# A layer's up and down products by seven: PSUM tiles of their own, a pinned matmul order, and another order of the seven

## The chip, the cores and the metric

The kernel runs on one core of a Trainium2 chip. Its time is the device time in microseconds (us) of one launch, and the median over runs counts.

## The reference

One step of a one-layer encoder on 576 tokens (a prompt of 512 and a sample of 64 with a cache of 128 rows), D_MODEL = 1024, D_FF = 4096, all in float32:

```python
def finish_layer(x, mix, pe, w_o, ln1_g, ln1_b, w_up, w_down, ln2_g, ln2_b, w_ple, w_ple_gate, b_ple_gate):
    x = layer_norm(ALPHA * x + jnp.einsum('blm,md->bld', mix, w_o), ln1_g, ln1_b)
    hid = jnp.square(jax.nn.relu(jnp.einsum('bld,df->blf', x, w_up)))
    x = layer_norm(ALPHA * x + jnp.einsum('blf,fd->bld', hid, w_down), ln2_g, ln2_b)
    gate = jax.nn.sigmoid(jnp.einsum('bld,de->ble', x, w_ple_gate) + b_ple_gate)
    return x + gate * jnp.einsum('blp,pd->bld', pe, w_ple)
```

`mix` comes from two kinds of attention over a joint projection of x; the change does not touch them. What it touches is the first layer norm and the two large products of the feed-forward part, w_up and w_down.

## The kernel before, in words

**Engines.** TensorE (PE) multiplies, VectorE (DVE) and ScalarE (ACT) do the steps between, SyncE (SP) issues most loads, GpSimd (POOL) some loads and a few sums. A float32 product is made of three matmuls in a rounded format: high part by high part, high by low, low by high. So each weight goes from its raw tile (`wraw`) into a tile `whl` with a high part, cast by ACT (line 149), and a low part, raw minus high, by DVE (line 155). The `whl` tiles are a ring of five slots. A slot is taken again when the weights that it held have been used.

**Stages.** Projection, attention, output product (`wo1`, `wo2`), first layer norm, up group 0 and 1 by plain products, then the phase of this change, `seven(todo)`, then a plain down part, the second layer norm and the gate. In PSUM there are eight banks: two tiles of two banks with tag "m" (pool psM), one tile of two banks with tag "g" (psB), and two banks of the pool psN.

**The seven-product phase.** Tokens are cut in two halves A and B of HW = 288 columns, the contracted dimension in two, the outputs in two. By a scheme like Strassen's, a block product that needs eight multiplications is made with seven, on sums and differences of the operands. The seven are called 11, t0, t1, 21, t3, t2 and 22. Each is four blocks of the contracted dimension times three matmuls, so 12 matmuls of 128x128 by 288 columns, and each has its own operand (`ROWS`: t0 uses the set s3, t1 s2, t3 s1, 21 the set 12, t2 the set 22, 22 the set s4). The sets of the hidden values lie in tiles hA (s3 and 11), hB (12 and 22), hC (s1 and s2) and hD (s4); `operands` makes them from hF and r (lines 1326 to 1356). A pair of output blocks runs through all seven:

- o = 11, then + t1, then + t2, in one accumulation;
- d begins as a copy of o after 11 (ACT, line 1466), then + 21;
- e begins as minus o after t1 (ACT, line 1468), then + t3 and + 22;
- z = t0.

DVE and ACT then add these into Y (a down pair, lines 1551 to 1571) or make relu and square of them (an up pair, lines 1524 to 1543). A pair's weights are four units u0 to u3 in four `whl` slots, two products to a slot except the last (`PLACE`): 11 and 21 in u0, t0 and t3 in u1, t1 and t2 in u2, 22 in u3. DVE makes the sums of raw weights (lines 181 and 184).

The list `todo` has 24 pairs in six stages of four: down (group 1), up (2 and 3), down (3), up (4 and 5), down (5), up (6 and 7). Together 24 × 7 × 12 = 2016 matmuls.

**PSUM in the phase.** o and z are the two banks of one tile `P.oz`: alternately the psN tile N2 and the psB tile. d and e are the two banks of a psM tile `P.sz`. The source's order in a pair is t0, t1, 21, t3, t2, 11 of the next pair, 22.

**What sets the order.** The source writes steps as generators; small work on ACT and DVE is put in a list (`later`, `owe`) and taken between matmuls. A scheduler then orders each engine's instructions by priorities and a cost model, and keeps the source's order only for instructions that are marked with `tc.keep_in_program_order`. Before, no matmul of `gemm` is marked.

Of the kernel before, what the change touches and what calls it, by code (L numbers as in the profile page):

```python
# [31 lines left out]
HW = NT // 2  # L32
# [4 lines left out]
def tile_hybrid_step(ctx: ExitStack, tc: tile.TileContext, I, O):  # L37
    nc = tc.nc
    PE, ACT, DVE, POOL, SP = nc.tensor, nc.scalar, nc.vector, nc.gpsimd, nc.sync
# [67 lines left out]
    class Unit:  # L107


        def __init__(self, t, c, o=0):  # L110
            self.t, self.c, self.o = t, c, o
# [166 lines left out]

    WT = Weights()

    def gemm(ps, W, kmap, aH, aL, cols, yield_every=6, first=True, last=True, wc=slice(0, 128), k0=0, more=False):

        n = len(kmap) * 3
        i = 0
        for kw, ka in enumerate(kmap, k0):
            for w, a in ((0, aH), (0, aL), (1, aH)):
                PE.matmul(ps, W(w, kw, wc), a[:, ka, cols], start=(first and i == 0), stop=(last and i == n - 1),  # L287
                          skip_group_check=more)
                i += 1
                if i % yield_every == 0:  # L290
                    yield 1
# [5 lines left out]
    psM = ctx.enter_context(tc.tile_pool(name="psM", bufs=1, space=PS))  # L297
# [56 lines left out]
    U = {}  # L354
# [355 lines left out]
    def proj_evac(p, kind, m):  # L710
        g, pp = divmod(p, 4)
        v = m[:, :, :HW]
        P = pair[p]
        dly = [0]

        def q(fn, d=None):
            if d is not None:
                dly[0] = d
            later(dly[0], fn)
# [5 lines left out]
        if kind == "v":  # L725
            v32 = sb.tile([128, NT], F32, name="v32", tag="t1")
            q(lambda: ACT.copy(v2(v32), v))
            P["v32"] = v32
            return
        QE = sb.tile([128, NT], F32R, name=kind + "E", bufs=2)  # L730
        QO = sb.tile([128, NT], F32R, name=kind + "O", bufs=2)
        P[kind + "E"], P[kind + "O"] = QE, QO
        sc = -0.125 if kind == "q" else 1.0
        if g == 0:
            if kind == "q":
                P["q32s"] = QS[p % 2]
                P["Q2"] = Q2[p % 2]

# [333 lines left out]
    for x, tag in ((0, "k32"), (1, "t2")):  # L1072
        t = sb.tile([128, NT], F32, name="praw", tag=tag)
# [34 lines left out]
    psN = ctx.enter_context(tc.tile_pool(name="psN", bufs=1, space=PS))  # L1108
    psB = ctx.enter_context(tc.tile_pool(name="psB", bufs=1, space=PS))
# [8 lines left out]
    turn = [0]  # L1118
# [4 lines left out]
            return psB.tile([128, 2, 512], F32, name="g", tag="g", bufs=1)  # L1123
        return psM.tile([128, 2, 512], F32, name="g", tag="m", bufs=2)

    N2 = psN.tile([128, 2, 512], F32, name="n", tag="n", bufs=1)
    turn_n = [0]

    def psum_n():
        turn_n[0] ^= 1  # L1130
        return N2[:, turn_n[0]]

    unit_w = WT.use

# [310 lines left out]
    ROWS = {"11": "11", "t3": "s1", "t0": "s3", "21": "12", "t1": "s2", "22": "s4", "t2": "22"}  # L1445

    def seven(pairs):

        def product(P, n):
            if n == "11":  # L1450
                P.oz = N2 if P.i % 2 == 0 else psB.tile([128, 2, 512], F32, name="g", tag="g", bufs=1)
            elif n in P.starts:
                P.starts[n]()
            x = P.X[ROWS[n]]
            while owed.get(ROWS[n]) and P.X is HX:
                pop_now()
            bank = {"11": (P.oz, 0), "t1": (P.oz, 0), "t2": (P.oz, 0), "t0": (P.oz, 1)}.get(n)
            t, o = bank or (P.sz, 0 if n == "21" else 1)
            ps, first = t[:, o, :HW], n in ("11", "t0")
            W = WT.quarter(P.u, n, oldest[0])  # L1460
            for _ in gemm(ps, W, range(4), x[0], x[1], slice(0, HW), first=first, more=not first):
                WT.step()
                yield 1
            if n == "11":
                P.sz = psM.tile([128, 2, 512], F32, name="g", tag="m", bufs=2)
                ACT.copy(P.sz[:, 0, :HW], ps)
            elif n == "t1":
                ACT.mul(P.sz[:, 1, :HW], ps, -1.0)  # L1468
            if n in P.posts:
                P.posts[n]()  # L1470
            for k, name in (("21", 1), ("t3", 2), ("t2", 3), ("22", 4)):
                if n == k:
                    oldest[0] = P.u + name

        oldest = [pairs[0].u]
        yield from product(pairs[0], "11")
        for i, P in enumerate(pairs):
            names = ["t0", "t1", "21", "t3", "t2", "22"]
            names.insert(1 if i == 0 else 5, "11")
            for n in names:  # L1480
                if n != "11":
                    yield from product(P, n)
                elif i + 1 < len(pairs):
                    yield from product(pairs[i + 1], n)

    class Pair:

        made = 0

        def __init__(self, u, X):  # L1490
            self.u, self.X, self.i = u, X, Pair.made
            self.starts, self.posts, self.left = {}, {}, 0
            Pair.made += 1
# [12 lines left out]
    def v2(G):  # L1506
        return G[:, :, :HW]

    def up_pair(g, m):

        P = Pair(U["P", g // 2, g % 2 * 2 + m], SX)
        b = slice(2 * m, 2 * m + 2)
        tt = DVE.tensor_tensor
        if m == 0:
            P.starts["t0"] = lambda: sets(g)

        def bank(n):
            return {"o": P.oz[:, 0, :HW], "z": P.oz[:, 1, :HW], "d": P.sz[:, 0, :HW], "e": P.sz[:, 1, :HW]}[n]

        def target(t):  # L1520
            return HX["f"][:, t, b] if g < G_DOWN and g % 2 == 0 else P.r[:, t]

        def t0():
            P.r = fs.tile([128, 2, 2, HW], F32, name="r", bufs=2)
            owe(P, lambda: ACT.copy(P.r[:, 1, 0], bank("z")))  # L1525

        def t3():
            settle(P)
            tt(P.r[:, 1, 1], bank("e"), P.r[:, 1, 0], OP.subtract)

        def t2():
            tt(P.r[:, 1, 0], bank("o"), P.r[:, 1, 0], OP.add)
            later(0, lambda: ACT.activation(P.r[:, 1], P.r[:, 1], AF.Relu))
            later(0, lambda: ACT.activation(target(1), P.r[:, 1], AF.Square))
            operands(g, m, 1, target(1))

        def s22():
            if g % 2:
                later(0, lambda: DVE.tensor_scalar(P.r[:, 0], v2(P.sz), 0.0, None, op0=OP.max))
            else:  # L1540
                later(0, lambda: ACT.activation(P.r[:, 0], v2(P.sz), AF.Relu))
            later(0, lambda: ACT.activation(target(0), P.r[:, 0], AF.Square))
            operands(g, m, 0, target(0))
        P.posts = {"t0": t0, "t3": t3, "t2": t2, "22": s22}
        return P

    def down_pair(g, c):

        P = Pair(U["Q", g // 2, c], HX)
        tt, stt = DVE.tensor_tensor, DVE.scalar_tensor_tensor  # L1550
        s = ALPHA if g == 1 else 1.0
        ya, y01, y11 = Y[:, 2 * c:2 * c + 2, A], Y[:, 2 * c, B], Y[:, 2 * c + 1, B]

        def begin(y, ps, op):
            if s == 1.0:
                tt(y, y, ps, op)
            else:
                stt(y, y, s, ps, op0=OP.mult, op1=op)

        def t0():  # L1560
            owe(P, lambda: begin(y01, P.oz[:, 1, :HW], OP.add))
            owe(P, lambda: begin(y11, P.oz[:, 1, :HW], OP.subtract))

        def t3():
            settle(P)
            tt(y11, y11, P.sz[:, 1, :HW], OP.add)

        def t2():
            later(0, lambda: tt(y01, y01, P.oz[:, 0, :HW], OP.add))

        def s22():
            later(0, lambda: begin(ya, v2(P.sz), OP.add))
        P.posts = {"t0": t0, "t3": t3, "t2": t2, "22": s22}
        return P

    def down_last(sl, ln):
# [223 lines left out]
```

## Time and profile before

| | us |
|---|---|
| median of 3 runs (lowest, highest) | 807.86 (807.19, 808.79) |
| profiled execution, its own time | 808.51 |
| its span | 806.7 |
| PE busy | 769.9 |
| DVE busy | 580.6 |
| ACT busy | 471.1 |
| POOL busy | 110.6 |
| seven-product phase, from 383.9 to 698.6 | 314.7 |

All times in views are from the span's start. A row of the timeline gives start, length, engine, line, operation, output and input, and how many instructions it groups. In square brackets is the idle time of the engine just ahead and what ended it. Rows of one engine overlap a little, since the end of an instruction lies behind the start of the next; what a step costs its engine is the distance from start to start.

### The profile page before, as it was taken

Reading aid. Unit: us, or ns where it says so; the run is one execution under the profiler, and the core shown is the slowest. Engines: PE = TensorE matmul, PEld = TensorE weight load, DVE = VectorE, ACT = ScalarE, POOL = GpSimd, SP = SyncE. Lnnn points to the kernel's source line nnn. Section 1 sums busy time; section 2 is a strip of 40 time slices with the busy share of each in tenths; the row PEclk is TensorE's granted clock in tenths of the full one; section 3 lists DMA queues with packets and bytes.
Section 4 is the critical chain, followed back from the end, with each engine's and each line's share of the span. In section 5 each row is a group of like instructions: output and inputs, shape, how many; then the busy total and the mean of one; then the engine's idle time right before and its main releaser. Section 6 shows DMA issues by size and latency. Waiting matters only on the chain.

```text
span 806.7 us, 14678 instructions
## 1 busy us (share of the span) xinstructions
PE 769.9 (95%) x5679; PEld 740.1 (92%) x5679; DVE 580.6 (72%) x1146; ACT 471.1 (58%) x927; POOL 110.6 (14%) x130
## 2 busy tenths in 40 slices
PE   9999999999999999999799997999979999999997
PEld 7999989989999999899699997999969999999997
DVE  6788898797778669986575678656795666558753
ACT  5689777877767343975433575435763365634552
POOL 7001324334420001000000000000000000010100
PEclk9999999999999999999799998999999999999999
DMA  8547444363233232536065664567554763651001
GB/s 277 167 60 174 118 120 124 96 200 107 84 87 100 74 123 103 193 75 149 0 161 131 166 165 110 125 151 182 146 131 101 174 162 91 243 183 53 28 27 66
DMA packets 38198, 101.36 MB, mean 126 GB/s; under 512 B 6000, under 2 KB 10224, under 8 KB 38000
## 3 DMA queue, kind: packets, MB, share of 16 engines
q1 hardware_dynamic: 34384, 87.61, 35.4%
q0 software_dynamic: 3456, 12.58, 9.7%
q8 instruction: 45, 0.74, 0.4%
q10 hardware_dynamic: 288, 0.22, 0.1%
q14 instruction: 25, 0.20, 0.1%
HBM read 85.26 MB, written 9.54 MB: 118 GB/s over the span
## 4 chain that ended last, share of the span: by engine, by line
PE 74%; DVE 14%; ACT 9%; issue 3%; DMA 1%; ACTq 0%; DVEq 0%
PE g L287 42%; PE m L287 14%; PE n L287 8%; ACT whl L149 2%; PE T L56 2%; PE V L955 2%; DVE dbias L690 2%; ACT xr L768 1%; DVE m L688 1%; DVE whl L155 1%; PE m L449 1%; PE S L880 1%; PE S L878 1%; DVE sP L888 1%; PE m L463 1%
## 5 line engine op out<-in xcount | busy, mean ns | idle before, releaser
L155 DVE TENSOR_TENSOR whl<-wraw,whl 128x1024 fp32r<-128x1024 f32 (+2 forms) x158 | 158.5, 1012 | 110.7 <-ACT whl L149 109.8
L149 ACT CAST whl<-wraw 128x1024 fp32r<-128x1024 f32 (+2 forms) x190 | 155.1, 828 | 114.7 <-PE g L287 89.9
L287 PE MATMUL g<-BH,whl 128*128 128x288 f32 (+2 forms) x864 | 181.4, 298 | 0.7 <-ACT whl L149 0.4
L287 PE MATMUL m<-AH,whl 128*128 128x288 f32 x736 | 176.7, 307 | 0.0
L287 PEld LDWEIGHTS g<-BH,whl 128*128 128x128 f32 x864 | 140.9, 188 | 3.7 <-ACT g L1468 2.5
L287 PE MATMUL g<-BL,whl 128*128 128x288 f32 (+2 forms) x432 | 127.6, 295 | 1.5 <-DVE BL L1221 1.5
L287 PEld LDWEIGHTS m<-AH,whl 128*128 128x128 f32 x736 | 126.4, 188 | 1.7 <-issue 1.0
L287 PE MATMUL m<-AL,whl 128*128 128x288 f32 x368 | 108.7, 295 | 0.0
L287 PEld LDWEIGHTS g<-BL,whl 128*128 128x128 f32 x432 | 81.4, 188 | 2.1 <-DVE BL L1221 2.0
L287 PEld LDWEIGHTS m<-AL,whl 128*128 128x128 f32 x368 | 69.5, 189 | 0.6
L210 POOL DMA_DIRECT2D wraw<-in_w_dram x24 | 20.7, 863 | 326.9 <-DMA wraw<-in_w_dram 219.7
L893 ACT ACTIVATE sP<-sP,st 128x128 f32<-128x128 f32 (+4 forms) x72 | 39.4, 550 | 35.4 <-DVE st L888 35.3
L155 POOL TENSOR_TENSOR whl<-wraw,whl 128x512 fp32r<-128x512 f32 x32 | 42.2, 1334 | 90.2 <-ACT whl L149 74.9
L287 PE MATMUL g<-s,whl 128*128 128x288 f32 x288 | 42.4, 296 | 0.8 <-ACT r L1525 0.8
L287 PE MATMUL m<-BH,whl 128*128 128x288 f32 x192 | 42.9, 302 | 0.0
L287 PE MATMUL g<-hB,whl 128*128 128x288 f32 x216 | 36.9, 325 | 6.3 <-ACT g L1468 6.3
L287 PEld LDWEIGHTS g<-hB,whl 128*128 128x128 f32 x216 | 33.2, 211 | 9.4 <-ACT g L1468 9.4
L287 PEld LDWEIGHTS g<-s,whl 128*128 128x128 f32 x288 | 39.3, 188 | 1.6 <-ACT r L1525 1.5
L287 PE MATMUL g<-hC,whl 128*128 128x288 f32 x216 | 34.6, 306 | 0.0
L56 PE MATMUL T<-ident,sP 128*128 128x128 f32 (+1 forms) x176 | 31.3, 273 | 1.5 <-DVE sP L902 0.6
L287 PEld LDWEIGHTS m<-BH,whl 128*128 128x128 f32 x192 | 32.0, 188 | 0.5 <-issue 0.3
L287 PEld LDWEIGHTS g<-hC,whl 128*128 128x128 f32 x216 | 31.5, 198 | 0.6
(329 smaller groups left out, 1567.7 us busy)
## 6 DMA issues: line engine op xcount, KB each, us to landing
wraw<-in_w_dram SPq DMA_DIRECT2D x48, 512.0 KB, 3.6
wraw<-in_w_dram POOLq DMA_DIRECT2D x24, 512.0 KB, 5.7
wraw<-in_w_qkv_dram SPq DMA_DIRECT2D x23, 512.0 KB, 3.6
wraw<-in_w_dram SPq DMA_DIRECT2D x24, 256.0 KB, 4.1
wraw<-in_w_up_dram SPq DMA_DIRECT2D x8, 512.0 KB, 4.4
wraw<-in_w_down_dram SPq DMA_DIRECT2D x8, 512.0 KB, 4.2
wraw<-in_w_gate_dram SPq DMA_DIRECT2D x8, 512.0 KB, 4.5
wraw<-in_w_o_dram SPq DMA_DIRECT2D x8, 384.0 KB, 3.1
```

Of the source, the lines that this page charges most:

```text
L56: PE.transpose(out, in_, ident[:n, :n])
L149: ACT.copy(self.hv[u][:, 0, c], src["tile"][:, c])
L155: eng.tensor_tensor(t[:, 1, c], src["tile"][:, c], f(t[:, 0, c]), OP.subtract)
L210: POOL.dma_start(t[:, :n], it["acc"], accum_op=OP.add)
L287: PE.matmul(ps, W(w, kw, wc), a[:, ka, cols], start=(first and i == 0), stop=(last and i == n - 1), skip_group_check=more)
L449: PE.matmul(mk[:, h, :HW], w0(part, k), a[:, k, h * HW:(h + 1) * HW], start=(k == 0 and i == 0), stop=(k == 7 and i == 2))
L463: PE.matmul(acc[b][:n[b], :304], a[:, k, b * 128:b * 128 + n[b]], ixw(part, k), start=(k == 0 and i == 0), stop=(k == 7 and i == 2))
L688: tc.keep_in_program_order(DVE.max(m, s))
L690: tc.keep_in_program_order(DVE.match_replace(out=s, in_to_replace=m, in_values=s, imm_value=GONE))
L768: q(lambda r=r, s=s: ACT.mul(v2(xr[r * 32:r * 32 + 32]), v[s * 32:s * 32 + 32], sc))
L893: ACT.activation(j["P"], j["P"], AF.Exp, bias=j["st"][:, 0:1], scale=-1.0, accum_out=j["st"][:, 2:3])
L955: PE.matmul(ps[r, x * 256 + c.start:x * 256 + c.stop], P["vt"][:, kb, r], t[:, hh, kb, c], start=(kb == 0), stop=(kb == n - 1))
```

## The change

Four things, all in the feed-forward part:

1. The matmuls of the seven-product phase are marked to stay in the source's order (`pin=True`).
2. Each of o, z, d, e gets its own place. o is a tile of one bank from psN (two of them, `psum_n`), z is bank 0 of the psB tile. In most pairs d and e are still the two banks of a psM tile. In a "turn" pair, the first of each down stage, d is the second bank of the psB tile and e the second bank of the psM tile, and d is added into Y after 21, without waiting for 22.
3. The source's order of the seven becomes 21, t1, 11 of the next pair, t3, t2, t0 of the next pair, 22; in a turn pair 11 of the next, t1, 21, t3, t2, t0 of the next, 22. The first pair begins with 11 and t0.
4. In odd up groups relu and square behind t2 are one DVE instruction (line 1529 in the new program) in place of two on ACT, and relu behind 22 is on ACT where it was on DVE.

The first layer norm uses `psum_n` too, so its sums lie in two tiles of one bank where they were the two halves of one tile.

```diff
-    def gemm(ps, W, kmap, aH, aL, cols, ..., k0=0, more=False):
+    def gemm(ps, W, kmap, aH, aL, cols, ..., k0=0, more=False,
+             pin=False):
...
-                PE.matmul(ps, W(w, kw, wc), a[:, ka, cols], ...)
+                mm = PE.matmul(ps, W(w, kw, wc), a[:, ka, cols], ...)
+                if pin:
+                    tc.keep_in_program_order(mm)
...
-    N2 = psN.tile([128, 2, 512], F32, name="n", tag="n", bufs=1)
-    turn_n = [0]
     def psum_n():
-        turn_n[0] ^= 1
-        return N2[:, turn_n[0]]
+        return psN.tile([128, 512], F32, name="n", tag="n", bufs=2)
...
         def product(P, n):
             if n == "11":
-                P.oz = N2 if P.i % 2 == 0 else psB.tile([128, 2, 512], F32, name="g", tag="g", bufs=1)
-            elif n in P.starts:
-                P.starts[n]()
+                P.o = psum_n()[:, :HW]
+            if n == ("11" if P.turn else "t0"):
+                P.g = psB.tile([128, 2, 512], F32, name="g", tag="g", bufs=1)
+                P.z = P.g[:, 0, :HW]
...
-            for _ in gemm(ps, W, range(4), x[0], x[1], slice(0, HW), first=first, more=not first):
+            for _ in gemm(ps, W, range(4), x[0], x[1], slice(0, HW), first=first, more=not first, pin=True):
...
             if n == "11":
-                P.sz = psM.tile([128, 2, 512], F32, name="g", tag="m", bufs=2)
-                ACT.copy(P.sz[:, 0, :HW], ps)
+                P.m = psM.tile([128, 2, 512], F32, name="g", tag="m", bufs=2)
+                P.d, P.e = P.g[:, 1, :HW] if P.turn else P.m[:, 0, :HW], P.m[:, 1, :HW]
+                ACT.copy(P.d, P.o)
             elif n == "t1":
-                ACT.mul(P.sz[:, 1, :HW], ps, -1.0)
+                ACT.mul(P.e, P.o, -1.0)
...
         yield from product(pairs[0], "11")
+        yield from product(pairs[0], "t0")
         for i, P in enumerate(pairs):
-            names = ["t0", "t1", "21", "t3", "t2", "22"]
-            names.insert(1 if i == 0 else 5, "11")
+            if P.start:
+                P.start()
+            for n in ("11+", "t1", "21", "t3", "t2", "t0+", "22") if P.turn else ("21", "t1", "11+", "t3", "t2", "t0+", "22"):
...
         def t2():   # up pair
-            tt(P.r[:, 1, 0], bank("o"), P.r[:, 1, 0], OP.add)
-            later(0, lambda: ACT.activation(P.r[:, 1], P.r[:, 1], AF.Relu))
-            later(0, lambda: ACT.activation(target(1), P.r[:, 1], AF.Square))
+            tt(P.r[:, 1, 0], P.o, P.r[:, 1, 0], OP.add)
+            if g % 2:
+                later(0, lambda: DVE.scalar_tensor_tensor(target(1), P.r[:, 1], 0.0, P.r[:, 1], op0=OP.max, op1=OP.mult))
+            else:
+                later(0, lambda: ACT.activation(P.r[:, 1], P.r[:, 1], AF.Relu))
+                later(0, lambda: ACT.activation(target(1), P.r[:, 1], AF.Square))
...
-        P = Pair(U["Q", g // 2, c], HX)
+        P = Pair(U["Q", g // 2, c], HX, c == 0)
...
+        def s21():  # down pair
+            if P.turn:
+                later(0, lambda: begin(ya[:, 0], P.d, OP.add))
         def s22():
-            later(0, lambda: begin(ya, v2(P.sz), OP.add))
+            if P.turn:
+                later(0, lambda: begin(ya[:, 1], P.e, OP.add))
+            else:
+                later(0, lambda: begin(ya, v2(P.m), OP.add))
```

How this moves instructions shows in the built programs (no times are in them). First PE in a steady down pair of the first down stage, before; x11 stands for eleven like it, hC is the set of t1 and t3, hB that of 21 and t2, hD that of 22, g_5010 the tile of o and z, g_5030 that of d and e:

```order
L287 MATMUL g_5010<-hC_4847,whl_5107 128x288 [waits DVE_49]
L287 MATMUL g_5010<-hC_4847,whl_5107 128x288 x5
L287 MATMUL g_5030<-hB_4694,whl_4996 128x288 [waits Activation_49]
L287 MATMUL g_5030<-hB_4694,whl_4996 128x288 x11
L287 MATMUL g_5030<-hC_4847,whl_5077 128x288 x12
L287 MATMUL g_5010<-hB_4694,whl_5107 128x288 x12
L287 MATMUL g_5030<-hD_4969,whl_5116 128x288 [waits DVE_49]
L287 MATMUL g_5030<-hD_4969,whl_5116 128x288 x11
```

The six rows of t1's second half are followed at once by 21, which waits for ACT (the copy of line 1468 into the other bank of its tile), then t3, t2 and 22. The same place after the change; n_5165 is this pair's o, n_5280 the next pair's, and g_5182 the tile of d and e:

```order
L288 MATMUL n_5165<-hC_4852,whl_5225 128x288 [waits Activation_49]
L288 MATMUL n_5165<-hC_4852,whl_5225 128x288
L288 MATMUL n_5165<-hC_4852,whl_5225 128x288 [waits DVE_49]
L288 MATMUL n_5165<-hC_4852,whl_5225 128x288 x9
L288 MATMUL n_5280<-hA_4429,whl_5271 128x288 [waits DVE_49,Activation_49]
L288 MATMUL n_5280<-hA_4429,whl_5271 128x288
L288 MATMUL n_5280<-hA_4429,whl_5271 128x288 [waits DVE_49]
L288 MATMUL n_5280<-hA_4429,whl_5271 128x288 x9
L288 MATMUL g_5182<-hC_4852,whl_5173 128x288 [waits Activation_49]
L288 MATMUL g_5182<-hC_4852,whl_5173 128x288 x11
L288 MATMUL n_5165<-hB_4699,whl_5225 128x288 x12
```

Behind t1 now stands the whole 11 of the next pair, with waits for its weights (ACT for the high part, DVE for the low part), and the wait for ACT's copy is at t3, twelve matmuls later.

Second, the head of the second down stage on PE, before; g_5793 is the last up pair's 22, hA holds the operands of 11 and t0 of the down pairs:

```order
L287 MATMUL g_5793<-BH_1145,whl_5812 128x288
L287 MATMUL n_4074<-hA_5445,whl_5894 128x288 x9
L287 MATMUL n_4074<-hC_5782,whl_5932 128x288 x6
L287 MATMUL g_6032<-hA_5445,whl_5979 128x288 x12
L287 MATMUL n_4074<-hC_5782,whl_5932 128x288 x6
```

After:

```order
L288 MATMUL g_5776<-BH_1145,whl_5834 128x288
L288 MATMUL n_5979<-hA_5474,whl_5981 128x288 x12
L288 MATMUL n_5891<-hC_5814,whl_5954 128x288 x12
L288 MATMUL g_5892<-hB_5716,whl_5881 128x288 x12
L288 MATMUL g_5909<-hC_5814,whl_5900 128x288 x12
```

Before, most of t0 (whl_5894) follows the 22, and the second pair's 11 (g_6032) stands between two halves of t1. After, t0 stands ahead of that 22 and the second pair's 11 (whl_5981) right behind it. whl_5981 is in the ring's slot that 22 (whl_5834) has just used, and ACT's cast into it waits for that 22.

Third, DVE at the same place, before:

```order
L1539 TENSOR_SCALAR r_5837<-g_5793 128x576
L155 TENSOR_TENSOR whl_5979<-wraw_5849,whl_5979 128x1024
L1349 SCALAR_TENSOR_TENSOR hF_5446<-hF_5446,r_5837 128x576
L1351 TENSOR_TENSOR hF_5446<-hF_5446,r_5837 128x576
L1326 TENSOR_TENSOR hB_5684<-r_5837,hB_5684 128x576
L1326 TENSOR_TENSOR hC_5782<-hF_5446,hC_5782 128x576 x2
L1326 TENSOR_TENSOR hB_5684<-r_5837,hB_5684 128x576
L1556 TENSOR_TENSOR Y_2745<-Y_2745,n_4074 128x288
L1356 TENSOR_TENSOR r_5837<-r_5837,hF_5446 128x576
L1556 TENSOR_TENSOR Y_2745<-Y_2745,n_4074 128x288
```

After:

```order
L1527 TENSOR_TENSOR r_5827<-n_5759,r_5827 128x288
L1529 SCALAR_TENSOR_TENSOR r_5827<-r_5827 128x576
L155 TENSOR_TENSOR whl_5965<-wraw_5865,whl_5965 128x512
L1348 SCALAR_TENSOR_TENSOR hF_5475<-hF_5475,r_5827 128x576
L1350 TENSOR_TENSOR hF_5475<-hF_5475,r_5827 128x576
L1551 TENSOR_TENSOR Y_2745<-Y_2745,g_5892 128x288
L1325 TENSOR_TENSOR hC_5814<-hF_5475,hC_5814 128x576
L1551 TENSOR_TENSOR Y_2745<-Y_2745,g_5892 128x288
L155 TENSOR_TENSOR whl_5954<-wraw_5738,whl_5954 128x1024
L1325 TENSOR_TENSOR hC_5814<-hF_5475,hC_5814 128x576
L1325 TENSOR_TENSOR hB_5716<-r_5827,hB_5716 128x576
L155 TENSOR_TENSOR whl_5981<-wraw_5870,whl_5981 128x1024
```

Before, the low part of the second pair's 11 (whl_5979) stood second and PE's first half of t1 waited for the two steps on Y (line 1556) behind the sums. After, the steps on Y (now line 1551) come from z in a tile of its own, and the low part (whl_5981) stands twelfth, behind the square, three sums of hF and hC and two other weights.

More of the change, by code (lines that the diff above doesn't have):

```diff
@@ L279, in tile_hybrid_step, with gemm @@
     WT = Weights()
-    def gemm(ps, W, kmap, aH, aL, cols, yield_every=6, first=True, last=True, wc=slice(0, 128), k0=0, more=False):
+    def gemm(ps, W, kmap, aH, aL, cols, yield_every=6, first=True, last=True, wc=slice(0, 128), k0=0, more=False,
+             pin=False):
         n = len(kmap) * 3
@@ L286, in gemm @@
             for w, a in ((0, aH), (0, aL), (1, aH)):
-                PE.matmul(ps, W(w, kw, wc), a[:, ka, cols], start=(first and i == 0), stop=(last and i == n - 1),
-                          skip_group_check=more)
+                mm = PE.matmul(ps, W(w, kw, wc), a[:, ka, cols], start=(first and i == 0), stop=(last and i == n - 1),
+                               skip_group_check=more)
+                if pin:
+                    tc.keep_in_program_order(mm)
                 i += 1
@@ L1450, in product @@
             if n == "11":
[L1451 to L1454 removed]
+                P.o = psum_n()[:, :HW]
+            if n == ("11" if P.turn else "t0"):
+                P.g = psB.tile([128, 2, 512], F32, name="g", tag="g", bufs=1)
+                P.z = P.g[:, 0, :HW]
             while owed.get(ROWS[n]) and P.X is HX:
                 pop_now()
[L1457 to L1459 removed]
+            x = P.X[ROWS[n]]
+            ps = P.o if n in ("11", "t1", "t2") else P.z if n == "t0" else P.d if n == "21" else P.e
+            first = n in ("11", "t0")
             W = WT.quarter(P.u, n, oldest[0])
[L1461 removed]
+            for _ in gemm(ps, W, range(4), x[0], x[1], slice(0, HW), first=first, more=not first, pin=True):
                 WT.step()
@@ L1464, in product, with __init__ @@
             if n == "11":
-                P.sz = psM.tile([128, 2, 512], F32, name="g", tag="m", bufs=2)
-                ACT.copy(P.sz[:, 0, :HW], ps)
+                P.m = psM.tile([128, 2, 512], F32, name="g", tag="m", bufs=2)
+                P.d, P.e = P.g[:, 1, :HW] if P.turn else P.m[:, 0, :HW], P.m[:, 1, :HW]
+                ACT.copy(P.d, P.o)
             elif n == "t1":
-                ACT.mul(P.sz[:, 1, :HW], ps, -1.0)
+                ACT.mul(P.e, P.o, -1.0)
             if n in P.posts:
                 P.posts[n]()
-            for k, name in (("21", 1), ("t3", 2), ("t2", 3), ("22", 4)):
-                if n == k:
-                    oldest[0] = P.u + name
+            if n in last_use:
+                oldest[0] = P.u + last_use[n]
+        last_use = {"21": 1, "t3": 2, "t2": 3, "22": 4}
         oldest = [pairs[0].u]
         yield from product(pairs[0], "11")
+        yield from product(pairs[0], "t0")
         for i, P in enumerate(pairs):
-            names = ["t0", "t1", "21", "t3", "t2", "22"]
-            names.insert(1 if i == 0 else 5, "11")
-            for n in names:
-                if n != "11":
+            if P.start:
+                P.start()
+            for n in ("11+", "t1", "21", "t3", "t2", "t0+", "22") if P.turn else ("21", "t1", "11+", "t3", "t2", "t0+", "22"):
+                if n[-1] != "+":
                     yield from product(P, n)
                 elif i + 1 < len(pairs):
-                    yield from product(pairs[i + 1], n)
+                    yield from product(pairs[i + 1], n[:2])
     class Pair:
[L1488 to L1493, printed above, removed]
+        def __init__(self, u, X, turn=False):
+            self.u, self.X, self.turn = u, X, turn
+            self.start, self.posts, self.left = None, {}, 0
     def owe(P, fn):
@@ L1514, in up_pair @@
         if m == 0:
-            P.starts["t0"] = lambda: sets(g)
-        def bank(n):
-            return {"o": P.oz[:, 0, :HW], "z": P.oz[:, 1, :HW], "d": P.sz[:, 0, :HW], "e": P.sz[:, 1, :HW]}[n]
+            P.start = lambda: sets(g)
         def target(t):
@@ L1524, in t0 @@
             P.r = fs.tile([128, 2, 2, HW], F32, name="r", bufs=2)
-            owe(P, lambda: ACT.copy(P.r[:, 1, 0], bank("z")))
+            owe(P, lambda: ACT.copy(P.r[:, 1, 0], P.z))
         def t3():
             settle(P)
-            tt(P.r[:, 1, 1], bank("e"), P.r[:, 1, 0], OP.subtract)
+            tt(P.r[:, 1, 1], P.e, P.r[:, 1, 0], OP.subtract)
         def t2():
-            tt(P.r[:, 1, 0], bank("o"), P.r[:, 1, 0], OP.add)
-            later(0, lambda: ACT.activation(P.r[:, 1], P.r[:, 1], AF.Relu))
-            later(0, lambda: ACT.activation(target(1), P.r[:, 1], AF.Square))
+            tt(P.r[:, 1, 0], P.o, P.r[:, 1, 0], OP.add)
[4 more added lines that the diff above has]
+                later(0, lambda: ACT.activation(target(1), P.r[:, 1], AF.Square))
             operands(g, m, 1, target(1))
         def s22():
[L1538 to L1541, printed above, removed]
+            later(0, lambda: ACT.activation(P.r[:, 0], v2(P.m), AF.Relu))
             later(0, lambda: ACT.activation(target(0), P.r[:, 0], AF.Square))
```

10 lines of the change are left out of this document (5 added, 5 removed).

## The prediction, made before the changed kernel ran

> **What bounds the kernel now.** I read the page's totals first, then TensorE (PE) by stage, then its waits, then PE's timeline at the places where it waits.
>
> ```profile
> span 806.7 us, 14678 instructions
> PE 769.9 (95%) x5679; PEld 740.1 (92%) x5679; DVE 580.6 (72%) x1146; ACT 471.1 (58%) x927; POOL 110.6 (14%) x130
> ```
>
> PE is the bound: 769.9 of 806.7 us. So the change can gain only PE's idle time and time that PE lost to a lower clock. The next view cuts the seven-product phase into its six stages, PE alone: stretch, length, PE busy, matmuls, granted clock, DMA share, GB/s. Stages one, three and five are down products (D1, D2, D3), the others up products (U1, U2, U3).
>
> ```profile
> 383.90:698.60 314.70, 290.89 (x2031) 0.96 0.54 135
> 383.90:444.10 60.20, 53.30 (x355) 0.91 0.40 100
> 444.10:494.50 50.40, 48.93 (x353) 1.00 0.64 160
> 494.50:547.40 52.90, 46.86 (x320) 0.94 0.54 128
> 547.40:597.80 50.40, 48.96 (x354) 1.00 0.64 158
> 597.80:650.30 52.50, 46.43 (x320) 0.93 0.54 129
> 650.30:698.60 48.30, 46.40 (x335) 1.00 0.52 140
> ```
>
> The down stages have the lost clock: 0.91, 0.94, 0.93 against 1.00. What PE waits for, over the whole span (us in total, times, longest):
>
> ```profile
> PE n L287 <- DVE Y L1556: 7.8, 2, 3.9
> PE g L287 <- ACT g L1468: 6.3, 12, 0.5
> PE n L287 <- DVE Y L1558: 4.3, 2, 3.7
> PE g L287 <- DVE BL L1221: 1.5, 1, 1.5
> ```
>
> Three are large: one long wait at the head of each down stage (L1558, then L1556 twice) and a short one at each of the twelve down pairs (L1468, the negated sum that opens the second bank). A steady down pair on PE (start, length, work, matmuls, idle before):
>
> ```profile
> 411.14 1.06 PE L287 MATMUL g<-hC,whl 128*128 128x288 f32 x6
> 412.73 1.85 PE L287 MATMUL g<-hB,whl 128*128 128x288 f32 x12 [0.53 <-ACT g L1468]
> 414.42 1.76 PE L287 MATMUL g<-hC,whl 128*128 128x288 f32 x12
> 416.02 1.76 PE L287 MATMUL g<-hB,whl 128*128 128x288 f32 x12
> ```
>
> Unhindered, twelve matmuls take 416.02 − 414.42 = 1.60 us, 0.133 each. By that measure the phase's 2031 matmuls need 270.8 us and it takes 314.7: 43.9 us are lost. By stage, in the same way: D1 12.9, U1 3.3, D2 10.2, U2 3.2, D3 9.8, U3 3.6 (windows cut at the edges, sum 43.0). In the steady pair, t1's six matmuls from 411.14 would let the next begin at 411.94; it began at 412.73, and another 0.09 went in that product (1.69 for 1.60): 0.9 us a pair.
>
> The heads of the down stages, D1's with two matmul groups broken by waits, D2's and D3's with one:
>
> ```profile
> 388.32 1.48 PE L287 MATMUL g<-hA,whl 128*128 128x288 f32 x10
> 393.49 1.78 PE L287 MATMUL n<-hC,whl 128*128 128x288 f32 x6 [3.69 <-DVE Y L1558]
> 395.90 1.78 PE L287 MATMUL n<-hC,whl 128*128 128x288 f32 x6 [0.64 <-DVE Y L1558]
> 494.54 1.59 PE L287 MATMUL g<-hA,whl 128*128 128x288 f32 x10 [0.30 <-DVE whl L155]
> 500.05 1.78 PE L287 MATMUL n<-hC,whl 128*128 128x288 f32 x6 [3.91 <-DVE Y L1556]
> 597.88 1.59 PE L287 MATMUL g<-hA,whl 128*128 128x288 f32 x10 [0.30 <-DVE whl L155]
> ```
>
> After 3.69 and 3.91 us of nothing, six matmuls take 1.78 us where six at full rate took 1.06: the clock has fallen. The granted clock, by one microsecond:
>
> ```profile
> 499.00:500.00 1.00, 0.00 (x0) 0.61 0.00 0
> 506.00:507.00 1.00, 1.00 (x10) 0.98 0.07 16
> 601.00:602.00 1.00, 0.00 (x0) 0.81 0.52 98
> 608.00:609.00 1.00, 1.00 (x8) 0.78 0.00 0
> ```
>
> At D2 it falls inside 499 and is back by 506, at D3 from inside 601 to inside 608: taking a window's mean for a mixture of full and half, 499.2 or later to some 506.4, and 601.6 to 608.45: about 6.8 us at half rate, worth 3.4 less the idle in it. D2's head so costs 3.9 + 0.3 + 3.2 = 7.4.
>
> **The change, part by part.**
>
> Own PSUM tiles and the new order in steady down pairs. Before, 21 stands right behind t1 and waits for the sign-changed copy (L1468) that writes another bank of the same tile. After, t1 is followed by twelve matmuls of the next pair's 11 (1.60 us), and only t3 needs that copy, which before let PE go 0.8 us behind t1's end. What covers it is that 11; if its weights were late, PE would wait there instead. 22 then follows t2 and the next t0, 3.2 us behind t3, so its wait for VectorE's (DVE's) use of t3 is covered too. The 0.9 at nine pairs that are not at a head gives 8.1 us; I take 0 for what is left, and it could be no less. The up pairs lose 3.3, 3.2, 3.6 before; I keep 1.5, 1.5 and 0.2: the first product of the next down stage still needs a weight (the cast queues behind two ScalarE (ACT) instructions, 0.55 + 0.93), and behind the last up stage ordinary products follow.
>
> Do the next pair's weights come in time? ACT casts the high part, DVE subtracts for the low:
>
> ```profile
> 384.11 0.65 ACT L1373 ACTIVATE r<-g 128x576 f32<-128x576 f32 x1 [0.44 <-PE g L287]
> 384.66 1.04 ACT L149 CAST whl<-wraw 128x1024 fp32r<-128x1024 f32 x1
> 385.60 0.68 ACT L1374 ACTIVATE r<-r 128x576 f32<-128x576 f32 x1
> 386.18 0.40 ACT L1466 COPY g<-n 128x288 f32<-128x288 f32 x1
> 385.73 1.23 DVE L155 TENSOR_TENSOR whl<-wraw,whl 128x1024 fp32r<-128x1024 f32 x1 [0.67 <-ACT whl L149]
> 386.87 0.75 DVE L1349 SCALAR_TENSOR_TENSOR hF<-hF,r 128x576 f32<-128x576 f32 x1
> 387.54 0.75 DVE L1326 TENSOR_TENSOR hB<-r,hB 128x576 fp32r<-128x576 f32 x1
> 392.89 0.45 DVE L1558 SCALAR_TENSOR_TENSOR Y<-Y,n 128x288 f32<-128x288 f32 x1
> 393.25 0.69 DVE L181 TENSOR_TENSOR wraw<-wraw 128x512 f32<-128x512 f32 x1
> ```
>
> From start to start: relu 0.55, cast 0.94, DVE's weight step 1.14, a 576-wide step 0.67, a 288-wide one 0.36. A slot comes free when the pair before ends with 22. Then 0.2 to begin, 0.94 and 1.15 make 2.3 to 2.4 us; the low part is due after 21, t1 and two matmuls of 11, 26 × 0.133 = 3.47. Margin 1.1 in down pairs; in up pairs a relu goes ahead and leaves 0.3 to 0.5. So zero, with little room there.
>
> Head of D1. By the new order of ACT and DVE, 11's copy (L1466) stands behind casts (1.1 idle), one 0.3 wait stays, and 21's evacuation stands behind three low steps of the sums (1.95): 3.35 us in three pieces. Whether the clock falls over these is open: I count half of 3.4, 1.7.
>
> Heads of D2 and D3. The slot of whl_5981, for the second pair's 11, is freed by the last up pair's 22, which now stands just ahead of it on PE. Counting from t2's end: t0 and 22 take 3.2, the cast lets 11 begin at 4.45 (1.25 idle), two matmuls need only the high part (to 4.7). The low part stands behind 8.0 us of DVE work: in the listed order six steps of 576 (4.0), three of 288 (1.1), one weight step of 512 (0.6, half of 1.14 and something to start) and, with itself, two of 1024 (2.3). With 0.3 more until PE answers, as in the row at 494.54, it goes on at 8.3: 3.6 idle. Together 4.85, and then half clock, at 2.0 (as the fall follows later) to 3.4, taken as 2.7. That is 7.5 against 7.4: no gain here. A wait for data (L1556) is replaced by one for weights.
>
> The rest. The fused DVE square (L1529) takes two ACT steps of 0.6 away at each odd up pair and adds 0.67 on DVE in place of the relu that ACT gets; both lie beside PE's work, and are in the queues above. The first pair's t0 now precedes t1: same instructions. No weight's DMA is added, removed or moved past another on SP's or POOL's queues; DMA share is 0.64 at most. PSUM tiles of the first layer norm: its sum no longer shares a tile with the row scale, so the transposes of that scale issue some 40 PE rows earlier, and DVE's steps behind it too.
>
> ```profile
> 329.89 0.42 PE L287 MATMUL g<-BH,whl 128*128 128x288 f32 x2
> 331.81 0.40 PE L287 MATMUL g<-BL,whl 128*128 128x288 f32 x1 [1.50 <-DVE BL L1221]
> ```
>
> Two matmuls from 329.89 leave PE free at 330.15, and it went on at 331.81. With the chain some 3 us earlier that 1.66 goes, and 0.2 of small gaps behind it: 1.9. Nothing else becomes late there that I can see; bounds 0 and 1.9.
>
> **The sum.** After, the phase loses D1 3.35 + 1.7, U1 1.5, D2 7.5, U2 1.5, D3 7.5, U3 0.2 = 23.25 us. The profiled execution took 808.51: 808.51 − 43.9 + 23.25 − 1.9 = 785.96. It lies 0.65 above the median of the runs (807.86), so against that 785.3. Bounds of the unknown: heads of D2 and D3 between 4.85 and 8.25 each, D1 between 3.35 and 6.75, layer norm 0 to 1.9: 778 to 791.
>
> **Rivals.**
>
> Full clock at the heads (B): the idle time is now in pieces, at D2 and D3 1.25 and 3.6 with two matmuls between, at D1 none above 2. If it never falls, D1 costs 1.7 and D2, D3 2.7 each less: 785.3 − 7.1 = 778.2. For it: no piece is longer than before's 3.69 to 3.91. Against it: at D3 PE's last matmul started its group at 597.88 and that ended by 599.47, and the clock fell at 601.6, 2.1 us later, so 3.6 is enough to be caught. [...]
>
> Weights late at the moved 11 (C): it now stands a product earlier, and the pin leaves PE nothing to take in its place. If casts or low steps run one 576 step (0.67) behind what I counted, up pairs lose 0.2 to 0.4, down pairs nothing; two behind, 0.9 to 1.0 and 0.25. Over eleven up and nine down steps that is 3 to 13 us: 788 to 798, say 793. For it: margin 0.3 to 0.5 in up pairs, DVE at 72% over the span. Against: DVE and ACT have fewer late steps there than I let stand ahead.
>
> Slower (D): the same mechanism at every step, where DVE's low part of the next 11's weights is late by a whole weight step behind others. The gain of 22.5 us spread over some 21 steps is 1.08 us: from a lateness of 2.2 us in down pairs and 1.5 in up pairs on, the change loses. At 0.2 us more a step it gives 812. Against: it takes two to three DVE steps of a kind that I did not find in the order.
>
> That nothing changes is excluded as far as order goes: PE's own order is another in all 24 pairs.
>
> **Chances.** Mine 0.53 (its own range 782 to 790), B 0.15, C 0.25, D 0.05, none of these 0.02. The median of runs of this kernel spreads by 0.2%, about what can be told from no change; that is 1.6 us, and 807.9 lies far from all but C's tail and D. So faster 0.91, same 0.03, slower 0.06. The range reaches from B to nearly all of C: 777.5 to 797.
>
> **What would show it.** Right: the L1468 wait gone, no wait by Y at L1556 or L1558 at the heads but weights (L155) of 3 to 4 us at two heads; stage lengths near 52 (D1), 48.6 (U1), 50 (D2), 48.7 (U2), 50 (D3), 45 (U3); the clock in up stages 1.00; the BL wait gone. Wrong: waits for L149 or L155 at each pair's 11, up stages above 50, heads with no half clock (B), or D1 with 1.00.

## The result, and the profile after

| | before | after |
|---|---|---|
| median us (lowest, highest) | 807.53 (805.98, 808.79) | 785.09 (783.34, 785.53) |
| ratio, 95% interval | | 0.9719 (0.9696 to 0.9742) |
| profiled execution, its own time | 808.51 | 783.34 |
| its span | 806.7 | 781.6 |
| seven-product phase | 383.91 to 698.61 | 382.23 to 672.79 |

The change gains 22.4 us, and 785.3 was forecast. The experiments will show that this number hides two effects of opposite sign. First the totals of the changed kernel, then its phase by stage (PE alone: length, busy, matmuls, clock, DMA share, GB/s), cut where the 22 of a stage's last pair ends, then its largest waits:

```profile
span 781.6 us, 14647 instructions
PE 755.0 (97%) x5679; PEld 734.4 (94%) x5679; DVE 581.2 (74%) x1149; ACT 465.5 (60%) x921; POOL 110.1 (14%) x130
```

```profile
382.23:672.79 290.56, 275.60 (x2027) 0.98 0.59 147
382.23:433.70 51.47, 48.42 (x363) 1.00 0.50 121
433.70:480.17 46.47, 45.08 (x338) 1.00 0.63 156
480.17:531.79 51.62, 47.05 (x338) 0.93 0.60 146
531.79:578.24 46.45, 45.06 (x338) 1.00 0.63 156
578.24:630.27 52.03, 47.47 (x338) 0.93 0.61 145
630.27:672.79 42.52, 42.52 (x323) 1.00 0.57 165
```

```profile
PE n L288 <- DVE whl L155: 8.3, 4, 3.4
PE n L288 <- ACT whl L149: 3.6, 4, 1.1
PE g L288 <- DVE Y L1553: 2.1, 1, 2.1
...
PE g L288 <- ACT g L1466: 1.0, 1, 1.0
```

These four lines are all the waits of the phase, ten of them. The twelve waits by line 1468 are gone. The pinned order lets whole products be counted: the stages hold 30, 28, 28, 28, 28 and 26 of 1.60 us each (the first two of D1 come ahead of its loop, and each stage does 11 and t0 of the next one's first pair). So D1, U1, D2, U2 and D3 lose 3.5, 1.7, 6.8, 1.7 and 7.2 us, together 20.9: 17.5 of it at the heads of the three down stages, and the rest where the next down stage's first 11 waits for its weights (0.66 and 0.73 us idle, near the end of U1 and of U2). U3 takes 0.9 more than its products, but no wait is in it: eight matmuls of the plain down part stand there, from 666.84 to 667.90. Outside the phase, the start is 1.68 us earlier, and the tail is 0.7 longer (108.8 for 108.1 us): before, 13 matmuls of the plain down part had been placed in the phase's last stage.

In a steady pair on PE, t2 follows t3 after 1.60 us:

```profile
404.96 1.77 PE L288 MATMUL g<-hC,whl 128*128 128x288 f32 x12
406.56 1.76 PE L288 MATMUL n<-hB,whl 128*128 128x288 f32 x12
```

The heads of D1 (two rows) and of D2 (four):

```profile
384.95 1.86 PE L288 MATMUL g<-hA,whl 128*128 128x288 f32 x12 [0.97 <-ACT g L1466]
...
392.08 1.87 PE L288 MATMUL g<-hB,whl 128*128 128x288 f32 x12 [2.08 <-DVE Y L1553]
```

```profile
481.47 0.53 PE L288 MATMUL n<-hA,whl 128*128 128x288 f32 x2 [1.14 <-ACT whl L149]
485.43 2.77 PE L288 MATMUL n<-hA,whl 128*128 128x288 f32 x10 [3.43 <-DVE whl L155]
487.99 2.45 PE L288 MATMUL n<-hC,whl 128*128 128x288 f32 x12
490.28 1.76 PE L288 MATMUL g<-hB,whl 128*128 128x288 f32 x12
```

At D2, two matmuls of the second pair's 11 run when the high part is there, and the other ten wait for the low part. That low part is DVE's twelfth step behind t2 (first and last of the twelve):

```profile
477.18 0.46 DVE L1527 TENSOR_TENSOR r<-n,r 128x288 f32<-128x288 f32 x1 [0.18 <-PE n L288]
...
484.16 1.22 DVE L155 TENSOR_TENSOR whl<-wraw,whl 128x1024 fp32r<-128x1024 f32 x1
```

From 477.18 the chain runs without a gap to 485.29. Then 22 matmuls take 4.85 us from 485.43 to 490.28 where 2.93 would do: half clock (granted 0.50 from 483 to 489), 1.9 us. D3 is the same, with 5.26 us from 583.50 to 588.76 (granted 0.50 from 582 to 588), 2.3 more than 2.93.

### The profile page after: what moved, and what is told of

The parts are those of the page before. It is cut to its first block, busy times and chain, and to the rows that moved or that the text cites. A ratio compares the mean times of both kernels' runs of the same rounds, so it can differ in the third digit from the quotient of the medians.

```text
span 781.6 us, 14647 instructions
## 1 busy us (share of the span) xinstructions
PE 755.0 (97%) x5679; PEld 734.4 (94%) x5679; DVE 581.2 (74%) x1149; ACT 465.5 (60%) x921; POOL 110.1 (14%) x130
## 4 chain that ended last, share of the span: by engine, by line
PE 76%; DVE 15%; ACT 7%; issue 2%; DMA 1%; ACTq 0%; DVEq 0%
PE g L288 40%; PE n L288 14%; PE m L288 13%; DVE dbias L693 2%; PE T L56 2%; ACT xr L771 2%; DVE whl L155 1%; DVE m L691 1%; ACT whl L149 1%; PE V L958 1%; PE m L452 1%; DVE sP L891 1%; PE m L466 1%; DVE x L774 1%; PE S L883 1%
## 5 line engine op out<-in xcount | busy, mean ns | idle before, releaser
L288 PE MATMUL g<-BH,whl 128*128 128x288 f32 (+2 forms) x768 | 157.6, 296 | 0.0
L288 PEld LDWEIGHTS g<-BH,whl 128*128 128x128 f32 x768 | 124.4, 188 | 0.4 <-DVE whl L155 0.2
L288 PE MATMUL g<-BL,whl 128*128 128x288 f32 (+2 forms) x384 | 113.0, 295 | 0.0
L288 PEld LDWEIGHTS g<-BL,whl 128*128 128x128 f32 x384 | 72.3, 188 | 0.2
L288 PE MATMUL n<-BH,whl 128*128 128x288 f32 x192 | 42.1, 295 | 0.0
L288 PE MATMUL n<-hA,whl 128*128 128x288 f32 x144 | 24.8, 322 | 11.9 <-DVE whl L155 8.3
L288 PEld LDWEIGHTS n<-hA,whl 128*128 128x128 f32 x144 | 21.9, 207 | 13.8 <-DVE whl L155 9.3
L288 PEld LDWEIGHTS n<-BH,whl 128*128 128x128 f32 x192 | 32.0, 188 | 0.0
```

The source lines that it names most:

```text
L288: mm = PE.matmul(ps, W(w, kw, wc), a[:, ka, cols], start=(first and i == 0), stop=(last and i == n - 1), skip_group_check=more)
```

## Experiments

The kernels before and after differ in three things that can be had apart: the tiles, the order of the seven in the source, and the pin. These runs make up a table of them (median us; each was timed against the kernel before, which stood at 807.8 to 808.4 in these comparisons). The rows with the new tiles also have the first norm's new tiles, worth 1.6 us, and the new square, whose worth can't be told from nothing (both below):

| tiles | order in the source | pin | us |
|---|---|---|---|
| old | old | no | 807.5 to 808.4 (before) |
| old | new, no turn | yes | 795.8 |
| old | new, no turn | no | 777.3 |
| new | old | no | 774.3 |
| new | old | yes | 785.5 |
| new | new, no turn | yes | 777.9 |
| new | new with turn | yes | 785.1 (the change) |
| new | new with turn | no | 771.2 |
| new | new, no turn | no | 770.4 |

**The order alone, pinned.** `product` keeps `P.oz` and `P.sz` as before, and the norm keeps N2; the pair's loop becomes

```diff
...
+            for n in ("21", "t1", "11+", "t3", "t2", "t0+", "22"):
...
```

> The kernel before with the new order of the seven (21, t1, 11 of the next, t3, t2, t0 of the next, 22, at every pair, no turn order) and the pin, but with the old PSUM tiles, in the norm too. Theory: the short waits by line 1468 need only the order, so they go (0.9 us at some nine pairs, 8 us), and the up stages lose 5 to 7 us less; the norm's wait (1.7) and one wait per down head of 4 us or more with half clock stay, since t1 still shares a tile with z. So about 793 us, 789 to 798. Rival, that the tiles carry the gain: 805 or more, with waits by line 1468 still listed at most down pairs.

Measured 795.79 (ratio 0.9847, 0.9826 to 0.9868): the time is as the theory said. From its waits:

```profile
PE g L288 <- ACT hB L1331: 8.9, 2, 4.5
...
PE n L288 <- DVE Y L1560: 4.3, 2, 3.4
```

There is no wait by the sign-changed copy: in steady pairs the order alone removes it. The wait at the heads is not quite the one that the theory named. Only at D1 does PE wait for Y (3.40 and 0.93 us); at D2 and D3 it stands 4.5 us before a 21 whose operand set 12 is not made.

**The tiles alone, not pinned.** The changed kernel with the old list of names, no turn pairs and no pin.

```diff
...
+            for n in (("t0", "11+") if i == 0 else ("t0",)) + ("t1", "21", "t3", "t2") + (("22",) if i == 0 else ("11+", "22")):
...
```

> The changed kernel's PSUM tiles (norm too) and its square, with the old order of the seven, no turn order and no pin. Theory: d and e still share one tile, and 21 stands right behind t1, so the twelve waits by line 1468 (0.5 us each) stay; what goes is the norm's wait (1.7) and at the heads part of the 4 us for Y, since z has a tile of its own: 796 to 803 us. Rival, that the tiles carry the gain: 790 or less.

Measured 774.33 (0.9581, 0.9567 to 0.9595): faster than the whole change. My theory fell, and so did the reading that 21 must wait behind t1. The order on PE shows why: with more tiles free, the scheduler put some of the next pair's 11 (here two matmuls of hA) between t1 and 21 by itself. One such place, then all waits of its phase:

```profile
399.30 0.42 PE L288 MATMUL n<-hA,whl 128*128 128x288 f32 x2
400.01 1.86 PE L288 MATMUL g<-hB,whl 128*128 128x288 f32 x12 [0.28 <-ACT g L1468]
```

```profile
PE n L288 <- ACT whl L149: 3.1, 4, 1.4
PE g L288 <- ACT g L1468: 2.2, 5, 0.7
```

Five waits of the old kind instead of twelve, and no wait for Y or for a low part.

**The change without its turn order.**

```diff
-        P = Pair(U["Q", g // 2, c], HX, c == 0)
+        P = Pair(U["Q", g // 2, c], HX)
```

> The changed kernel with the steady order at the first pair of each down stage too, d in the psM tile there. Theory: 21 of the first pair needs the set 12, which is made last (relu, square, cast, low part behind the last up pair's 22), so PE waits there some 5 us at once and the clock falls: heads cost 8 to 10 each, D1 too: 787 to 792 us. Rival, that the turn order brings nothing: within 1 us of the changed kernel's 785.

Measured 777.86 (0.9632, 0.9612 to 0.9653): neither the theory nor its rival. Pinned, the turn order costs some 7 us. The waits at the heads:

```profile
PE g L288 <- ACT hB L1327: 5.2, 2, 2.6
PE g L288 <- DVE hB L1325: 1.6, 3, 0.8
```

I had not seen that half of 21's operand comes from the up pair before the last, so that PE does six matmuls of it before it waits. And at D1, 21 first does not wait for the evacuation: PE's only wait there is 0.17 us for the set 12. The clock falls at D2 and D3 in this run too: the twelve matmuls of t1 behind that 21 take 2.88 and 2.46 us from start to start, at D1 1.60.

**The change without the pin.**

```diff
-            for _ in gemm(ps, W, range(4), x[0], x[1], slice(0, HW), first=first, more=not first, pin=True):
+            for _ in gemm(ps, W, range(4), x[0], x[1], slice(0, HW), first=first, more=not first):
```

> The changed kernel without the pin. The scheduler then puts other matmuls first at the heads of the down stages and leaves nearly all steady pairs as they are. Theory: the order written in the source carries the gain: 782 to 789 us. Rival, that the pin carries the gain: 795 or more.

Measured 771.22 (0.9542, 0.9527 to 0.9556), 14 us faster than with the pin. Both expectations fell: the pin carries no gain, it takes 14 us back. D2's head in this run:

```profile
477.01 0.42 PE L288 MATMUL n<-hC,whl 128*128 128x288 f32 x2
478.31 0.53 PE L288 MATMUL n<-hA,whl 128*128 128x288 f32 x2 [0.87 <-ACT whl L149]
478.68 0.96 PE L288 MATMUL g<-hB,whl 128*128 128x288 f32 x6
479.47 1.48 PE L288 MATMUL n<-hC,whl 128*128 128x288 f32 x10
481.43 0.40 PE L288 MATMUL g<-hB,whl 128*128 128x288 f32 x1 [0.47 <-ACT hB L1327]
482.43 1.59 PE L288 MATMUL n<-hA,whl 128*128 128x288 f32 x10 [0.60 <-DVE whl L155]
```

After the two matmuls of 11 (hA) come six of 21 and ten of t1, which are ready, and the other ten of 11 stand where their low part is due. The wait for the low part has gone from 3.43 to 0.60 us, all idle time of this head from 4.57 to 1.94, and the clock stays at 1.00 over the phase.

**The pin everywhere but at the heads.** In the first pair of each down stage no matmul is pinned; the built PE order differs from the changed kernel's there alone.

```diff
-            ... first=first, more=not first, pin=True):
+            ... first=first, more=not first, pin=not at[0]):
...
+            at[0] = P.turn
...
```

> The changed kernel with the pin taken off in the first pair of each down stage only. The built order differs from the changed one at those three heads alone, where it is the order of the kernel without a pin. Theory: all of the pin's cost lies at the three heads: 771 to 774 us, no wait over 1.2 us in the phase. Rival: the pin costs a little at each pair: 779 or more.

Measured 772.72 (0.9561, 0.9536 to 0.9586), as the theory said. So of the pin's 14 us, about 12 lie at the three heads; whether the other 1.5 is real these intervals do not tell.

**The order alone, not pinned.** The first of these kernels without its pin.

> The old PSUM tiles with the new order (no turn order) and no pin. Theory: without the pin the scheduler fills part of the heads, but t1 still has to wait until z is out of its tile, so one wait of some 3 us per down stage stays: 787 to 796 us. Rival, that the order alone, set free, does what the tiles do: 780 or less.

Measured 777.33 (0.9618, 0.9591 to 0.9645): the rival. A free order does nearly what the tiles do. The wait for Y that I thought unavoidable with z and t1 in one tile is

```profile
PE n L288 <- DVE Y L1558: 0.7, 2, 0.3
```

0.3 us at a head, where it had been 3.9 before. The shared tile did not make that wait long by itself. At D2 in the kernel before, nine of t0's matmuls on PE and then DVE's two additions of z; below them the additions in this run:

```profile
491.82 1.36 PE L287 MATMUL n<-hA,whl 128*128 128x288 f32 x9
...
498.42 0.45 DVE L1556 TENSOR_TENSOR Y<-Y,n 128x288 f32<-128x288 f32 x1
...
499.45 0.45 DVE L1556 TENSOR_TENSOR Y<-Y,n 128x288 f32<-128x288 f32 x1
```

```profile
480.87 0.45 DVE L1558 TENSOR_TENSOR Y<-Y,n 128x288 f32<-128x288 f32 x1
...
483.75 0.45 DVE L1558 TENSOR_TENSOR Y<-Y,n 128x288 f32<-128x288 f32 x1
...
484.78 1.42 DVE L1329 TENSOR_TENSOR hC<-hF,hC 128x576 fp32r<-128x576 f32 x2
```

Before, t0 stood mostly behind the last up pair's 22, and z, whole by some 493.2, was added from 498.42 on, behind the low parts of the sums. In the new order t0 stands ahead of that 22, and z is added ahead of hC's low parts, which t1 needs anyway.

**The old order with the new tiles, pinned.** The kernel with the tiles alone, and the pin.

> The new PSUM tiles with the old order of the seven (no turn order), pinned. Theory: pinned, 21 stands right behind t1 at each of 24 pairs and waits for the copy of line 1468 (0.5 to 0.8 us each), and the heads have nothing to put ahead: 12 to 25 us slower than the same without the pin (774.3), so 786 to 800. Rival: the pin is harmless and only the new order makes it dear: within 3 us of 774.

Measured 785.46 (0.9714, 0.9683 to 0.9745), half a microsecond below the theory's range. Its phase has one kind of wait:

```profile
PE g L288 <- ACT g L1468: 15.8, 23, 1.7
```

This is the reading from before in its pure form: 21 right behind t1, at 23 pairs. With the new tiles it holds only where a pin forbids anything else: without the pin, five such waits are left.

**The clock at the heads.** Repeats of the first matmul of the second pair's 11, with its start flag, at D2 and D3.

```diff
+            if n == "11" and P.fill:
+                for _ in range(FILL):
+                    tc.keep_in_program_order(PE.matmul(ps, W(0, 0, slice(0, 128)), x[0][:, 0, slice(0, HW)], start=True,
+                                                       stop=False, skip_group_check=True))
...
```

With FILL = 24:

> The changed kernel with 24 more matmuls at the heads of the second and third down stage: the first matmul of the second pair's 11 is repeated with its start flag, so the values stay the same, and PE is busy for 3.2 of the 3.43 us in which it waits for that pair's low weight part. In the changed kernel's trace the 22 matmuls behind that wait take 1.9 and 2.3 us longer than at full clock. Theory: the clock falls because PE is nearly idle over those 5 us, so with the repeats it stays at 1.00 there and the kernel gains 3.5 to 4.5 us: 780.5 to 782. Rival: the fall hangs on something else and the repeats are only more work: 785 or more.

Measured 778.77 (0.964, 0.9616 to 0.9664): the theory's cause, and some 2 us more gain than its range allows, which a fall of the clock at D1 in most executions of the changed kernel may explain (see the part on D1 below). The clock stays at 1.00 through both heads. But in its profiled execution (781.07, the others 778.6 to 778.8) the clock fell at D1, where the program is the changed kernel's. D1's wait, and the granted clock by one microsecond:

```profile
392.40 3.25 PE L288 MATMUL g<-hB,whl 128*128 128x288 f32 x12 [2.08 <-DVE Y L1560]
```

```profile
391.00:392.00 1.00, 0.00 (x0) 1.00 0.00 0
392.00:393.00 1.00, 0.60 (x2) 0.66 0.00 0
393.00:394.00 1.00, 1.00 (x6) 0.50 0.00 0
...
395.00:396.00 1.00, 1.00 (x7) 0.63 0.00 0
```

The same wait of 2.08 us was without a fall in the changed kernel's trace. With FILL = 10:

> The kernel with repeated matmuls at the heads of the second and third down stage, with 10 repeats in place of 24, so PE is idle some 1.1 us, busy 1.6, idle 2.1, at each of the two heads. Theory: idle pieces of about 2.1 us let the clock fall in some executions and not in others, as at the first head, where 2.08 us gave no fall in the changed kernel's trace and one in that with 24 repeats: single times spread from 778.6 to 783, in steps of about 2 us. Rival one, that any filling stops the fall: all within 1 us of 778.8 but for one more fall at the first head. Rival two, that the fall follows the mean of PE's work over these 5 us: all 782 or more.

Measured 780.9 (0.9672, 0.9651 to 0.9693), times 780.85, 780.89, 780.91, 782.46. The theory holds in kind, though the times spread less than it said, and this one trace has both cases: a wait of 2.11 at D2 with a fall, the same wait at D3 without (10 matmuls in 2.34 and in 1.59 us).

```profile
485.45 2.34 PE L288 MATMUL n<-hA,whl 128*128 128x288 f32 x10 [2.11 <-DVE whl L155]
...
583.22 1.59 PE L288 MATMUL n<-hA,whl 128*128 128x288 f32 x10 [2.11 <-DVE whl L155]
```

```profile
486.00:487.00 1.00, 1.00 (x6) 0.50 0.01 4
489.00:490.00 1.00, 1.00 (x7) 0.80 0.00 0
...
584.00:585.00 1.00, 1.00 (x10) 1.00 0.07 16
```

**The norm's tiles alone.** The kernel before, with one-bank tiles for the first norm and N2 allocated only when the norm is done.

```diff
+        if NN[0] is None:
+            return psN.tile([128, 512], F32, name="n", tag="n", bufs=2)
...
```

> The kernel before with separate one-bank tiles for the first layer norm alone (the seven-product phase has the old tiles and the old order on PE). Theory: PE's wait for BL (1.50 us) goes and the phase begins 1.4 to 1.9 us before 383.91, at 382.0 to 382.5; the rest of the time stays. Rival, that the norm's gain came by something else in the change: the phase begins within 0.3 us of 383.91.

One execution (807.87, span 806.1), so its time tells nothing beside runs that spread by 4 us, but its trace does:

```profile
330.62 0.51 PE L287 MATMUL g<-BH,whl 128*128 128x288 f32 x2
330.96 0.29 PE L287 MATMUL g<-BL,whl 128*128 128x288 f32 x1
...
382.30 1.75 PE L287 MATMUL n<-hA,whl 128*128 128x288 f32 x12
```

The wait for BL is gone and the phase begins at 382.30, 1.61 us earlier. The theory holds.

**The square as before.** Relu and square behind t2 on ACT, relu behind 22 on DVE in odd groups, in the changed kernel.

```diff
-            if g % 2:
-                later(0, lambda: DVE.scalar_tensor_tensor(target(1), P.r[:, 1], 0.0, P.r[:, 1], op0=OP.max, op1=OP.mult))
...
```

> The changed kernel with relu and square of odd up groups as before: two ACT steps behind t2, and relu behind 22 on DVE. Theory: both lie beside PE's work in the pairs, and DVE's chain ahead of the late weight at the two heads loses one step of 0.67 and may gain another: 783 to 787 us. Rival, that ACT needs the time: casts late at up pairs, 789 or more.

Measured 784.69 (0.9728, 0.9688 to 0.9767; one of its four executions took 789.05): no difference from the changed kernel that can be told. The waits only move: those for the low part are 2.6 us near the ends of U1 and U2 and 2.4 at the heads of D2 and D3, in place of 0.7 and 3.4. The clock falls at all four places: near the ends of U1 and U2 the ten matmuls behind the wait take 2.74 and 2.77 us, where they take 1.60 and 1.59 in the changed kernel, and at D2 and D3 the 22 behind it take 4.52 and 4.39, where 2.93 would do. In the changed kernel it falls at D2 and D3 only, for 6.8 us each.

**The best version.** Neither pin nor turn order.

> The changed kernel without the pin and with the steady order at the first pair of each down stage too. Theory: set free, the scheduler fills the heads by itself, so the turn order is worth little beside the pin: 770 to 774 us. Rival, that the turn order and d in a bank of its own are needed at the heads even then: 775 or more.

Measured 770.39 (0.9537, 0.9518 to 0.9556): 15 us faster than the change, and the same as without the pin alone within these intervals. The theory holds: where the order is free, the turn order is worth nothing that can be told.

## Why the prediction came out right, point by point

- **Steady pairs** (8.1 us to gain, nothing left): right in the trace, no wait by line 1468 and products of 1.60 us. But the prediction put tiles and order together as one remedy. They are two, and either does most of it alone: with the old tiles and the new order, free, 777.3; with the new tiles and the old order, free, 774.3.
- **Up stages** (1.5, 1.5 and 0.2 left): measured 1.7, 1.7 and nothing. The stage lengths that the prediction gave as signs (48.6 for U1, say) keep the cuts of before and cannot be laid beside the rows above, which cut elsewhere.
- **D1** (3.35 idle): 3.1, by its two waits of 0.97 and 2.08; 3.5 from start to start. The half of 3.4 for the clock was a guess over an open question. There was no fall in the profiled execution (783.34, mean granted clock 0.990), while the other three took 784.8 to 785.5 at 0.988. Half clock for 3.4 us takes 0.002 off the mean over 782 us, and with 24 repeats the fall at D1 made 2.3 us. So that these three had the fall fits, but no trace of them shows it.
- **D2 and D3** (4.85 idle and 2.7 for the clock, 7.5): measured 1.14 + 3.43 = 4.57 idle, clock 1.9 and 2.3, loss 6.8 and 7.2. The chain of 8.0 us on DVE, counted from the built order and durations of before, ran from 477.18 to 485.29, 8.1. One reading of the prediction on the clock before is off: a mean of 0.98 between 506 and 507 puts the end of D2's half clock at 506.04, not 506.4. The 6.8 us that it goes on with are those to 506.04.
- **Norm** (1.9): 1.68 here, 1.61 by itself.
- **The sum**: against the profiled execution 785.96 was forecast and 783.34 came; the median came within 0.2 us. The difference of the profiled one is 1.5 at D1 (5.05 forecast, 3.5 lost) and some 1 at D2 and D3; smaller terms of both signs cancel. So the 2.6 us tell how good the sum is. That the median hit so closely is luck: in the changed kernel it lies 1.75 us above the profiled execution, where 0.65 below was put in.

What the prediction did not do is price the pin as an edit of its own. It read the heads' 7.5 us as the cost of weights that arrive late. They do arrive late, but only because PE may not take anything else meanwhile does it cost that. The rival of late weights said that the pin leaves PE nothing to take in its place, and put the price at steady pairs; it is paid at the heads of the down stages. The full-clock rival did not come true: the clock fell at both heads, although no idle piece was longer than 3.43.

## What to carry to other kernels

When one edit brings a new order and fixes it, time the fixing apart: here 37 us were to be had, and the pin gave 14 of them back at three places that make up a small part of the phase. A wait that is read off one order shows what to free, but a scheduler that is allowed to may fill it by itself as soon as a tile or a place in the order is free; so the first experiment is the change without its constraint. And where a stall cannot go, filling it with work whose repetition changes no value may keep the clock, as it did here: 24 repeated matmuls at two heads took away both stretches of half clock, 4.2 us by the changed kernel's trace.

## What the runs showed of the hardware

A wait of 2.08 us brought half clock at D1 in one execution (24 repeats) and not in another (the changed kernel), and one of 2.11 us at D2 but not at D3 of one execution (10 repeats; rows above). With a mean between 0.50 and 1.00 taken as a mixture of full and half clock, the first of these falls came at 392.32, just before PE was at work again at 392.40, and ended at 395.74; the second came at 485.98 (0.99 between 485 and 486), half a microsecond after PE had resumed at 485.45, and ended at 489.40. Each lasted 3.4 us. In the changed kernel half clock lasted 6.8 us at D2, from 482.72, when PE had been idle for 0.7 us since its last matmul, to 489.54:

```profile
482.00:483.00 1.00, 0.00 (x0) 0.86 0.93 168
...
489.00:490.00 1.00, 1.00 (x7) 0.73 0.00 0
```

At D3 it went from 581.70 to 588.52, 6.8 us as well. In the kernel before it lasted 6.8 us at D2, from 499.22 to 506.04, and at D3, from 601.62 to 608.44, each beginning in a wait of 3.91 us; at D1, beginning in the wait of 3.69 us, it lasted 10.2 us, from 393.40 to 403.64:

```profile
393.00:394.00 1.00, 0.51 (x2) 0.70 0.00 0
...
403.00:404.00 1.00, 1.00 (x7) 0.68 0.00 0
```

What decides whether a wait of some 2.1 us brings a fall, and how long half clock then lasts, these runs do not show.
